# The divided input projection of a streaming encoder step: its two accumulators in PSUM tiles of their own

## Chip, cores and metric

One NeuronCore of one Trainium2 chip. The metric is the device time of one execution in microseconds (us).

## What is computed

One step of a one-layer encoder for 512 new frames of one stream (the prompt) and 32 frames of a running stream. All 544 frames go through the kernel together. The part that matters here is the input projection and the recurrence that it feeds:

```python
def token_mixer(x, s0, lat_past, kr_past, blk, lb, w_in, ...):
    proj = x @ w_in                                   # (544, 2048) @ (2048, 4928)
    hq, hf, hi, hg, cq, ckv, kr = jnp.split(proj, SPLITS, axis=-1)
    f = lb + (1.0 - lb) * jax.nn.sigmoid(hf.astype(jnp.float32))
    o_h, s_new = hgrn2_recurrence(heads(hq), heads(1.0 - f), heads(jnp.log(f)), heads(hi), s0, blk)
    o_h = rms_norm(o_h, ...) * jax.nn.silu(hg)
    ...                                               # MLA attention from cq, ckv, kr
    return jnp.concatenate([o_h, o_a], axis=-1) @ w_out, ...
```

Then follow layer norms and a ConvFFN with 5632 channels. There are eight heads of 128 columns in each of hq, hf, hi and hg. Everything is in fp32.

## The kernel before, in words

Every fp32 factor is split into a high part and a low part (`wh`, `wl` for weights; `aH`, `aL` or the pairs in `sums` for the activations), and a product is made of three matmuls: high by high, high by low, low by high. ACT makes the high part of a weight by a rounding copy, DVE the low part by a subtraction.

The projection of heads 0 and 1 is plain. Heads 2 to 7 use a divided form: a group `c` stands for 256 output columns (hq and hf of a head, or hi and hg of a head) and 544 frames. Columns, frames and the 2048 inner rows are each cut in two, and seven products of half size take the place of eight, in the order `ORDER = ("11", "s1", "s2", "s4", "s3", "12", "22")`. There are 12 groups and so 84 products. A product is 8 steps of k by 3 matmuls, each 128x128 weights by 272 columns (`NI`), all at line L773. Before some products DVE forms a difference of two raw weight blocks (`form`, L711); `begin` (L716, ACT) and `complete` (L721, DVE) make a product's high and low parts two products ahead.

The function `divided(c, a, b, after)` multiplies one group. It has two accumulators, x and y. Products 11, s2, s3 and 22 are added up in x, s1 and s4 in y, and 12 opens y afresh; the accumulator therefore alternates from product to product: x y x y x y x. After each product one 128x272 reading of its accumulator is needed (`take`): four of the seven are copies by ACT (L758), three are additions to what is there by DVE (L761), after which the forget gate or the output gate goes on (`after`, L789, L790, L798, L799). A `take` isn't issued at once. It is put in `later`, and `settle()` issues it in the middle of the next product, after its k = 3, just ahead of `complete`. After each half product the generator yields.

x and y are two slices of one tile of `main_tile()`: a tile of 128 x 1024 fp32 in the PSUM pool `psm`, which has two such tiles. Each group asks for a tile, so the groups take turns. The other PSUM of this stage is the pool `psg`: one tile `sw` of 1024 columns and two tiles `s1` of 512 columns, for the recurrence.

Between the half products ("slots") stand the steps of the recurrence, placed by `turns`: per head one generator `levels(h)` of nine steps and one `finish(h)` of eleven. `levels` begins with `Kp` and `Qp` on DVE (L815, L816), then the matmuls L821 (from `Kp`) and, level by level, L838 and L841 or L836 on PE, L842, L850 and L854 on DVE, L844 on POOL. `finish` has transposes and matmuls L870, L880, L892, L902, L904 on PE, L885, L887 and L894 on DVE, and at its end a chain: a square on ACT (L907), a sum and a scale on DVE (L911, L912), a power on POOL (L913), a multiplication on DVE (L916), five transposes on PE (L921), the result on DVE (L923, L925).

All this is inside `manual_schedule(engines=MANUAL)`: PE, DVE and ACT run their instructions in the order in which the code issues them. The framework puts in the semaphore waits. DMAs are issued on SP: four raw weight blocks of 512 KB for each group (L701). When the groups are over, `wo_tiles` takes two tiles of the same pool `psm` for the output projection (`out_first`, L118), whose instructions the framework places itself.

Of the kernel before, what the change touches and what calls it, by code (L numbers as in the profile page):

```python
# [42 lines left out]
NI = T // 2  # L43
# [16 lines left out]
def tile_encoder_step(ctx, tc, xp, xs, w_in, w_in4, w_kr, w_q_b, w_kv_b, w_out, w_up, w_gate, w_down, w_down2,  # L60
# [31 lines left out]
    def main_tile():  # L92
        return psm.tile([P, 1024], F32, name="main", tag="main")
# [54 lines left out]
    def pair_half(ps, j):  # L148
        n = H_[j].stop - H_[j].start
        return [ps[:, 512 * t:512 * t + n] for t in range(2)]  # L150
# [213 lines left out]
    with tc.tile_pool(name="mp", bufs=1) as mp, tc.tile_pool(name="psa", bufs=4, space=PSUM) as psa:  # L364
# [67 lines left out]
        c = {}  # L432
# [207 lines left out]
    with tc.tile_pool(name="gp", bufs=1) as gp, tc.tile_pool(name="psg", bufs=1, space=PSUM) as psg:  # L640
# [83 lines left out]
        def operand(name, k):  # L724
            if name in sums:
                return part(name, k, 0), part(name, k, 1)
            kg, j = {"11": (k, 0), "s3": (k, 1), "12": (HK + k, 0), "22": (HK + k, 1)}[name]
            return aH[kg][:, H_[j]], aL[kg][:, H_[j]]
# [4 lines left out]
        def begin(n):  # L733
            if n < len(products):
                ws_of[n] = products[n][0].high(products[n][1])

        def complete(n):

            if n < len(products):
                ws_of[n] = products[n][0].low(ws_of[n])  # L740
                if n + 1 < len(products):
                    products[n + 1][0].form(products[n + 1][1])

        def settle():
            now, later[:] = later[:], []
            for f in now:
                f()

        def divided(c, a, b, after):

            ps = main_tile()
            x, y = ps[:, :NI], ps[:, 512:512 + NI]
            t0, t1 = H_

            def take(name, out):
                kept = {"11": a[:, t0], "s1": b[:, t1], "s2": b[:, t0], "22": a[:, t1]}.get(name)
                if kept is not None:
                    A.activation(kept, out, AF.Copy)  # L758
                else:
                    z = {"s4": b[:, t0], "s3": b[:, t1], "12": a[:, t0]}[name]  # L760
                    V.tensor_tensor(out=z, in0=z, in1=out, op=ALU.add)  # L761
                    if name != "12":
                        after(z)

            for i, name in enumerate(ORDER):
                n = 7 * (c - N_PLAIN) + i
                begin(n + 2)
                wh, wl = ws_of.pop(n)
                out = x if name in ("11", "s2", "s3", "22") else y
                for k in range(HK):  # L770
                    oh, ol = operand(name, k)
                    for q, (ww, aa) in enumerate(((wh, oh), (wh, ol), (wl, oh))):
                        PE.matmul(out, ww[:, k * P:(k + 1) * P], aa, start=name in ("11", "s1", "12") and k == 0 and q == 0,  # L773
                                  stop=k == HK - 1 and q == 2, skip_group_check=True)
                    if k == 3:
                        settle()
                        complete(n + 2)
                        yield
                later.append(lambda name=name, out=out: take(name, out))
                yield  # L780
# [4 lines left out]
        def divided_qf(h):  # L785
            q, f = hq[h], hf[h] = proj_tile(), proj_tile()

            def forget(z):
                A.activation(z, z, AF.Sigmoid)  # L789
                A.activation(z, z, AF.Identity, bias=lb[:, h:h + 1], scale=oml[:, h:h + 1])  # L790
            yield from divided(2 * h, q, f, forget)

        def divided_ig(h):
            i, g = hi[h], hgate[h] = proj_tile(), proj_tile()

            def gate(z):
                e = gp.tile([P, 2, NI], F32, name="sg", tag="sg")[:, 0]
                A.activation(e, z, AF.Sigmoid)  # L798
                later.append(lambda: V.tensor_tensor(out=z, in0=z, in1=e, op=ALU.mult))  # L799
            yield from divided(2 * h + 1, i, g, gate)  # L800
# [143 lines left out]
        for n in range(2):  # L944
            begin(n)
            complete(n)
        last_finish = finish(HEADS - 1)
        with tc.manual_schedule(engines=MANUAL):

# [50 lines left out]
    def acc_tile():  # L1000
        seq[0] += 1
        if seq[0] % 2:
            return main_tile()
        return psA.tile([P, 1024], F32, name="acc", tag="acc")
# [349 lines left out]
    for g in (5, 6, 7):  # L1354
# [3 lines left out]
        if g < 7:  # L1358
            ps = pair_half(acc_tile(), 0)
# [218 lines left out]
    with tc.manual_schedule():  # L1578
# [26 lines left out]
        ps = pair_half(acc_tile(), 0)  # L1605
# [81 lines left out]
        for p in range(2, BP):  # L1687
            x = Pair(p)
# [553 lines left out]
```

## Time and profile before

| | |
|---|---|
| median of 3 runs | 2451.21 us (2450.78 to 2453.78) |
| the profiled execution | 2452.24 us, span 2450.5 us |
| PE busy | 2354.3 us (96% of the span) |
| DVE busy | 1812.1 us (74%) |
| ACT busy | 1045.2 us (43%) |
| POOL busy | 191.5 us (8%) |
| matmuls of L773 | 380.7 to 776.0 us |

How to read the rows: PE is TensorE's matmul, PEld its weight load, DVE is VectorE, ACT is ScalarE, POOL is GpSimd, SP issues the DMAs. A row of the timeline has the start in us, the length in us, engine, line, operation, what is written <- what is read, shapes and how many were merged; brackets hold the idle time of the engine ahead of it and what ended it. A row of waits reads "who <- for whom: total us, times, longest us". A row of the windows has, for a stretch of time, its length and then the busy time and number of instructions of PE, PEld, DVE, ACT and POOL, then the granted share of TensorE's clock, DMA's share and GB/s. Tile names are shown without numbers, so both tiles of `psm` are called `main`. Matmuls overlap: each row of L773 is some 0.29 us long, and the next begins some 0.13 us after it.

### The profile page before, as it was taken

To read this page: it belongs to the slowest core of one execution; us is meant where nothing else is said; L and a number is where in the kernel's file an instruction comes from. 1 tells how busy PE (TensorE), PEld (TensorE's weight loads), DVE (VectorE), ACT (ScalarE), POOL (GpSimd) and SP (SyncE) were. 2 spreads that over 40 slices of the span, in tenths; PEclk is the share of its full clock that TensorE was granted. 3 is DMA by queue.
4 is the path that set the end of the run, shared out by engine and by line. 5 is a ranking of instruction groups with operands and counts; after the bars stand their busy time and mean duration, and the time that the engine had idled before them with its cause. 6 is when DMAs were issued, how large, how long until landed. Compare 5 with 4: busy or idle time off the path is not lost.

```text
span 2450.5 us, 44455 instructions
## 1 busy us (share of the span) xinstructions
PE 2354.3 (96%) x18462; PEld 2317.5 (95%) x18462; DVE 1812.1 (74%) x2447; ACT 1045.2 (43%) x1615; POOL 191.5 (8%) x219
## 2 busy tenths in 40 slices
PE   6999999888899999989999999999999999999997
PEld 6999999888888999989999999999999999999996
DVE  7445577666667546799888888888777888888566
ACT  4244433333334224656555555555444433333234
POOL 4010020111111020000000000000000100000023
PEclk9999999999999999999999999999999999999998
DMA  7232163222224433644535253534333874633322
GB/s 231 91 97 65 62 200 95 70 77 69 73 76 145 170 101 124 204 135 161 174 119 184 102 191 112 177 127 164 117 117 118 313 300 170 224 133 94 115 70 74
DMA packets 131914, 333.21 MB, mean 136 GB/s; under 512 B 11904, under 2 KB 64896, under 8 KB 127104
## 3 DMA queue, kind: packets, MB, share of 16 engines
q1 hardware_dynamic: 122448, 286.91, 35.6%
q0 software_dynamic: 5040, 39.00, 4.0%
q10 hardware_dynamic: 4224, 4.46, 0.5%
q8 instruction: 145, 2.38, 0.4%
q14 instruction: 57, 0.47, 0.1%
HBM read 272.78 MB, written 56.15 MB: 134 GB/s over the span
## 4 chain that ended last, share of the span: by engine, by line
PE 75%; DVE 6%; ACT 2%; issue 2%; POOL 0%; DMA 0%; ACTq 0%; SPq 0%; DVEq 0%
PE main L1217 20%; PE acc L1217 16%; PE main L773 9%; PE main L1245 8%; PE main L118 7%; PE acc L1245 6%; PE acc L118 5%; PE s L838 1%; DVE wl L1169 1%; ACT hproj L758 1%; ACT wh L716 0%; DVE wl L721 0%; DVE hproj L761 0%; ACT zb L1337 0%; PE sw L902 0%
## 5 line engine op out<-in xcount | busy, mean ns | idle before, releaser
L1168 ACT ACTIVATE wh<-raw 128x1024 fp32r<-128x1024 f32 x340 | 359.9, 1059 | 415.0 <-DVE raw L1161 134.4
L1169 DVE TENSOR_TENSOR wl<-raw,wh 128x1024 fp32r<-128x1024 f32 x340 | 415.8, 1223 | 133.9 <-ACT wh L1168 133.0
L1217 PE MATMUL main<-op,wh 128*128 128x272 f32 x1408 | 265.7, 288 | 0.0
L1217 PE MATMUL acc<-ops,wh 128*128 128x272 f32 x1344 | 255.7, 289 | 4.3 <-DVE ops L1298 4.3
L1217 PE MATMUL main<-ops,wh 128*128 128x272 f32 x1344 | 254.2, 287 | 0.0
L1217 PEld LDWEIGHTS main<-op,wh 128*128 128x128 f32 x1408 | 221.0, 188 | 0.0
L1217 PEld LDWEIGHTS acc<-ops,wh 128*128 128x128 f32 x1344 | 212.1, 189 | 4.6 <-DVE ops L1298 4.6
L1217 PEld LDWEIGHTS main<-ops,wh 128*128 128x128 f32 x1344 | 211.0, 188 | 0.0
L1217 PE MATMUL main<-op,wl 128*128 128x272 f32 x704 | 203.1, 288 | 0.9 <-DVE wl L1169 0.9
L1217 PE MATMUL acc<-ops,wl 128*128 128x272 f32 x672 | 194.3, 289 | 0.0
L1217 PE MATMUL main<-ops,wl 128*128 128x272 f32 x672 | 193.8, 288 | 0.2 <-DVE wl L1169 0.2
L118 PE MATMUL main<-aL,wh 128*128 128x272 f32 (+2 forms) x768 | 180.1, 292 | 4.6 <-POOL aL L269 4.6
L118 PE MATMUL main<-aH,wh 128*128 128x272 f32 (+2 forms) x768 | 183.4, 296 | 1.1 <-ACT x L267 0.7
L118 PE MATMUL main<-aH,wl 128*128 128x272 f32 (+2 forms) x768 | 178.9, 291 | 0.0
L107 DVE TENSOR_TENSOR wl<-raw,wh 128x1024 fp32r<-128x1024 f32 (+2 forms) x80 | 89.9, 1127 | 102.9 <-ACT wh L106 97.9
L1217 PE MATMUL acc<-op,wh 128*128 128x272 f32 x832 | 159.8, 290 | 1.6 <-DVE eg L1441 1.6
L1168 ACT ACTIVATE wh<-rawl 128x1024 fp32r<-128x1024 f32 x93 | 98.5, 1060 | 105.8 <-DVE rawl L1161 42.1
L1161 DVE TENSOR_TENSOR raw<-raw,raw 128x1024 f32<-128x1024 f32 x114 | 139.2, 1221 | 1.8 <-DMA raw<-in_w_up 0.2
L773 PE MATMUL main<-aH,wh 128*128 128x272 f32 x384 | 118.2, 308 | 22.6 <-DVE hproj L761 22.6
L1169 DVE TENSOR_TENSOR wl<-rawl,wh 128x1024 fp32r<-128x1024 f32 x93 | 113.8, 1223 | 32.7 <-ACT wh L1168 32.4
L106 ACT ACTIVATE wh<-raw 128x1024 fp32r<-128x1024 f32 (+2 forms) x80 | 75.5, 949 | 140.2 <-PE acc L118 65.6
L118 PEld LDWEIGHTS main<-aL,wh 128*128 128x128 f32 x768 | 129.6, 191 | 5.8 <-POOL aL L269 5.7
(421 smaller groups left out, 6162.0 us busy)
## 6 DMA issues: line engine op xcount, KB each, us to landing
raw<-in_w_in SPq DMA_DIRECT2D x76, 512.0 KB, 3.6
raw<-in_w_up SPq DMA_DIRECT2D x72, 512.0 KB, 4.6
raw<-in_w_gate SPq DMA_DIRECT2D x72, 512.0 KB, 4.0
raw<-in_w_down SPq DMA_DIRECT2D x71, 512.0 KB, 4.1
raw<-in_w_out SPq DMA_DIRECT2D x40, 512.0 KB, 3.5
opd<-ohl SPq DMA_DIRECT2D x16, 1088.0 KB, 5.5
ops<-opd POOLq DMA_DIRECT2D x16, 1088.0 KB, 9.7
opd<-ohl SPq DMA_DIRECT2D x16, 816.0 KB, 6.4
```

The costliest lines, as they stand in the source:

```text
L106: A.activation(dst(hv), src(rv), AF.Copy)
L107: V.tensor_tensor(out=dst(lv), in0=src(rv), in1=dst(hv).bitcast(F32), op=ALU.subtract)
L118: PE.matmul(ps, ww[:, wcols[0]:wcols[1]], aa[:, hs[j]], start=first and i == 0, stop=last and i == 2, skip_group_check=True)
L758: A.activation(kept, out, AF.Copy)
L773: PE.matmul(out, ww[:, k * P:(k + 1) * P], aa, start=name in ("11", "s1", "12") and k == 0 and q == 0, stop=k == HK - 1 and q == 2, skip_g ...
L838: PE.matmul(ps[:, j * 64:(j + 1) * 64], Kp[:, a:b], Qv[:, j * bt:(j + 1) * bt, 1, :], start=True, stop=True)
L1161: V.tensor_tensor(out=out, in0=a, in1=b, op=ALU.subtract)
L1168: A.activation(wh, src, AF.Copy)
L1169: V.tensor_tensor(out=wl, in0=src, in1=wh.bitcast(F32), op=ALU.subtract)
L1217: PE.matmul(ps, ww[:, k * P:(k + 1) * P], aa, start=self.first and k == 0 and i == 0, stop=k == n - 1 and i == 2, skip_group_check=True)
L1245: PE.matmul(banks[:, 512 * u:512 * u + NI], ww[:, (u * n + k) * P:(u * n + k + 1) * P], aa, start=self.first and k == 0 and i == 0, stop=k ...
```

## The change

The two accumulators become the first 272 columns of two tiles. The tiles are asked for once, ahead of the first group, and kept for all of them. x of group c lies in tile c % 2 and y in the other one. As a group has seven products, the last of a group and the first of the next lie in different tiles.

```diff
@@ -748,8 +748,7 @@
 
         def divided(c, a, b, after):
 
-            ps = main_tile()
-            x, y = ps[:, :NI], ps[:, 512:512 + NI]
+            x, y = (banks[(c + i) % 2][:, :NI] for i in range(2))
             t0, t1 = H_
 
             def take(name, out):
@@ -944,6 +943,7 @@
         for n in range(2):
             begin(n)
             complete(n)
+        banks = [main_tile() for i in range(2)]
         last_finish = finish(HEADS - 1)
         with tc.manual_schedule(engines=MANUAL):
```

## The prediction

> **What bounds the kernel now.** I read the page first, then the stage in which the changed lines run, then its waits, then its timeline. The page:
>
> ```profile
> PE 2354.3 (96%) x18462; PEld 2317.5 (95%) x18462; DVE 1812.1 (74%) x2447; ACT 1045.2 (43%) x1615; POOL 191.5 (8%) x219
> ...
> PE main L1217 20%; PE acc L1217 16%; PE main L773 9%; PE main L1245 8%; PE main L118 7%; PE acc L1245 6%; PE acc L118 5%; PE s L838 1%; DVE wl L1169 1%; ACT hproj L758 1%; ACT wh L716 0%; DVE wl L721 0%; DVE hproj L761 0%; ACT zb L1337 0%; PE sw L902 0%
> ```
>
> PE is busy 96% of the span, so only its idle time or its work can be saved. The last of these lines is the chain of work that ended last: the multiplications of the divided projection (L773) hold 9% of it, and the two lines that empty their accumulators (L758 on ACT, L761 on DVE) stand in it too. An emptying line in this chain means that PE waited for it. The stage, from the view of busy time by windows, and then its waits (total, times, longest):
>
> ```profile
> core 0: us, PE busy (x) PEld busy (x) DVE busy (x) ACT busy (x) POOL busy (x), PEclk, DMA share, GB/s
> 380.70:776.00 395.30, 353.33 (x2749) 338.85 (x2748) 271.90 (x389) 143.44 (x214) 53.10 (x49) 0.99 0.27 83
> ```
>
> ```profile
> ACT hproj L758 <- PE main L773: 77.6, 26, 4.7
> DVE hproj L761 <- PE main L773: 25.1, 13, 4.3
> PE main L773 <- DVE hproj L761: 22.6, 23, 2.5
> PE main L773 <- ACT hproj L758: 17.9, 31, 1.0
> ```
>
> PE is idle for 395.30 - 353.33 = 42.0 us of the stage, and 22.6 + 17.9 = 40.5 us of that ends when L761 or L758 has read an accumulator: 54 stalls in 84 products. The other two rows show the reverse wait, of the reading engine for PE. One stall, in the timeline:
>
> ```profile
> 733.72 0.29 PE L773 MATMUL main<-aL,wh 128*128 128x272 f32 x1
> ...
> 733.84 0.29 PE L773 MATMUL main<-aH,wl 128*128 128x272 f32 x1
> 734.17 0.44 DVE L761 TENSOR_TENSOR hproj<-hproj,main 128x272 f32<-128x272 f32 x1 [4.23 <-PE main L773]
> 734.52 1.22 DVE L721 TENSOR_TENSOR wl<-raw,wh 128x1024 fp32r<-128x1024 f32 x1
> ...
> 734.66 0.39 PE L773 MATMUL main<-aH,wh 128*128 128x272 f32 x1 [0.53 <-DVE hproj L761]
> ```
>
> The row at 733.84 is the last matmul of a product's first half (k = 3). By the code the DVE row adds the accumulator of the product before, the other half of the same tile. It starts only when that first half ends, and PE's second half starts only when it is done. Neither touches the other's columns: x is in columns 0 to 271, y in 512 to 783. So the wait is one of the shared tile. The counterproof is the first product of a group, whose `settle` reads the old group's tile:
>
> ```profile
> 743.84 0.38 ACT L758 ACTIVATE hproj<-main 128x272 f32<-128x272 f32 x1
> 743.86 0.28 PE L773 MATMUL main<-aL,wh 128*128 128x272 f32 x1
> ```
>
> There ACT reads one `main` while PE writes another, and PE's row has no idle time ahead of it.
>
> **The change, part by part.** No instruction, DMA or wait on data is added or removed; the order on each engine's queue stays, since the stage is ordered by hand. Three things change.
>
> *1. The wait in the middle of a product goes.* The price of one: from 733.84 to 734.66 is 0.82 us where 0.13 is usual (733.72 to 733.84), so 0.69 is lost, 0.16 more than the 0.53 that counts as idle (a matmul's row is 0.29 long, but they start every 0.13). All 54 stalls: 40.5 + 54 x 0.16 = 49.1 us, the most that this can return.
>
> Not all of it returns, because PE then arrives early at other waits. The stage repeats with the heads, so I walk one head, from the matmuls L821 to the next head's L821:
>
> ```profile
> 683.63 0.60 PE L821 MATMUL sw<-hproj,Kp 128*128 128x128 f32 x4
> ...
> 749.39 1.20 PE L821 MATMUL sw<-hproj,Kp 128*128 128x128 f32 x10
> ```
>
> ```profile
> 683.60:749.40 65.80, 58.08 (x458) 55.66 (x457) 44.79 (x63) 22.39 (x33) 8.75 (x8) 1.00 0.22 67
> ```
>
> ```profile
> 740.44 0.40 PE L773 MATMUL main<-aH,wh 128*128 128x272 f32 x1 [2.51 <-DVE hproj L761]
> ...
> 747.78 0.52 PE L773 MATMUL main<-s,wh 128*128 128x272 f32 x2 [0.49 <-ACT hproj L758]
> ```
>
> Idle in this head: 65.80 - 58.08 = 7.72 us in ten stalls. The last three are those at 734.66, 740.44 and 747.78; the seven before them hold 7.72 - 0.53 - 2.51 - 0.49 = 4.19 idle, 4.19 + 7 x 0.16 = 5.3 lost. For these I find nothing that is late next. In the levels, where DVE has most to do, it waits for PE ahead of each level's product:
>
> ```profile
> 695.80 0.44 DVE L842 TENSOR_TENSOR Qp<-Qp,tot 128x272 f32<-128x272 f32 x1 [0.65 <-PE s L841]
> ...
> 700.77 0.44 DVE L842 TENSOR_TENSOR Qp<-Qp,tot 128x272 f32<-128x272 f32 x1 [1.74 <-PE s L841]
> ```
>
> Each of these waits shrinks by one stall (0.49 to 0.60 idle, 0.65 to 0.76 lost), and the smallest, 0.65, is just used up by it. If that cover were gone, a level would cost what DVE has too much. So 5.3 us return.
>
> The last three stalls, 3.53 idle and 4.0 lost, return only in part. Here DVE runs a chain of its own that ends in the next head's `Kp`, which L821 needs:
>
> ```profile
> 739.22 0.82 DVE L916 TENSOR_TENSOR sqg<-sw,r 128x640 f32<-128x640 f32 x1 [1.28 <-POOL r L913]
> ...
> 743.97 2.46 DVE L721 TENSOR_TENSOR wl<-raw,wh 128x1024 fp32r<-128x1024 f32 x2 [0.26 <-ACT wh L716]
> ...
> 747.48 0.44 DVE L815 TENSOR_SCALAR Kp<-hproj 128x544 f32<-128x544 f32 x1
> ```
>
> From the end of L916 (740.04) to the end of `Kp` (747.92) there are 7.88 us with one idle time, 0.26, in it; and L916 itself hangs on POOL and on a rounding (734.52) that follows the reading at 734.17 in the queue and so can start at most 0.35 earlier; I take 0.2. PE gets from L916's end to L821 in 749.39 - 740.04 = 9.35 us now, and after in no less than 7.88 + 0.05. So this end of the head returns 0.2 + 1.4 = 1.6 of 4.0 us. Late next are the transposes L921 (for L916, by about 1.2 us) and L821 (for `Kp`, by about as much).
>
> One head returns 5.3 + 1.6 = 6.9 us; the five alike (50 of the 54 stalls) 34.5. The other four stalls have 40.5 - 5 x 7.72 = 1.9 idle, 2.5 lost; of these 2.0 return. **Sum of part 1: 36.5 us.**
>
> *2. The same two accumulators serve every group.* A product's first matmul now waits for the reading of two products before, also across a group's end, where a fresh tile was taken. That reading is issued half a product earlier, 12 x 0.126 = 1.5 us ahead of the need, and no longer waits for PE. Where L921 stands at the group's end, ACT's reading (743.84 to 744.22) ends 4.2 us behind L916's end, held up in ACT's queue by a rounding that waits for DVE. PE would want that accumulator at 3.6 (L921, then 24 matmuls): 0.6 us of wait, but L821 has to wait for `Kp` anyway, so it costs nothing there. At the other group ends I count none. Bounds: nothing below, since a wait gains nothing; above, this line's one sequencer wait, for each of 84 products, 4.3 us:
>
> ```profile
> L773 PEldq EVENT_SEMAPHORE  x1: 51/51/51, 398.5 to 398.5; - x1
> ```
>
> I take 0, since the line's 54 waits of now made only this one such row.
>
> *3. The tiles after the stage.* The output projection's first tile was free early, and four of its matmuls filled PE before the stage had ended:
>
> ```profile
> L118 PE MATMUL main<-aH,wh x2: 290/340/390, 767.8 to 772.1; 128*128 128x272 f32 x2
> L118 PE MATMUL main<-aL,wh x2: 287/287/287, 772.2 to 772.3; 128*128 128x272 f32 x2
> ```
>
> Now the tile is held until the last group is read, and they follow. Cost at most 4 x 0.13 = 0.5 us, which I take. Weight loads follow the buffers' release, which comes earlier with the reading engines; DMA at a share of 0.27 covers them.
>
> **The clock.** Twice in the stage the granted clock halves after one of the 2.5 us stalls:
>
> ```profile
> 538.16:541.57 3.41, 1.58 (x12) 1.58 (x13) 2.77 (x4) 0.00 (x0) 0.57 (x1) 1.00 0.00 0
> 541.57:544.99 3.42, 3.42 (x18) 3.42 (x17) 2.83 (x5) 2.29 (x3) 0.00 (x0) 0.50 0.09 33
> 674.69:678.11 3.42, 3.42 (x18) 3.42 (x17) 2.81 (x5) 2.29 (x3) 0.00 (x0) 0.50 0.08 29
> ```
>
> PE was busy 1.58 of the 3.41 us before. Each half clock costs 3.42 / 2 = 1.7 us. With the long stall down to about 1.2 us no window of that length is half empty, so I take both as gone: 3.4 us. The Trainium skill, "TensorE: Matmul & The Clock Gate", section on the HAM clock gate, has the clock fall after an idle window of about 3.4 us; here it fell after a window with 1.58 us of work. By the page's rule these dips would not come from the stalls and would stay, the sum would be 36.0 and the time 2415; I go by the rows.
>
> **Sum.** 36.5 - 0.5 + 3.4 = 39.4 us. The profiled execution took 2452.24 us (span 2450.5), which gives 2412.8; the median of the runs shown, 2451.21, is 1.0 below it, so **2412 us** as the median.
>
> **Rivals.**
>
> *All of it returns* (49.1 + 3.4): about 2399. For it: L916 and `Kp` could come earlier if the readings ahead of them in DVE's queue shift more than I saw. Against it: the 7.88 us chain has 0.26 us of slack.
>
> *DVE is the bound wherever it ended a stall.* Then only ACT's stalls return, 17.9 + 31 x 0.16 = 22.9: 2428. For it: DVE is busy 271.9 of what would be about 356 us. Against it: the 1.74 us waits above, and 25.1 us in which DVE itself waits for the first halves.
>
> *The change doesn't do what it says*: the mid-product wait has another cause than the tile, and stays: 2451. Against it: the rows at 743.84.
>
> *Slower, by too few banks.* The stage falls from four halves of 512 columns in turn to two. If the readings come later than a product's start, every product waits. To lose, PE must wait more than 49.1 / 84 = 0.58 us on each of 84 products, that is, each reading must end over 1.5 + 0.58 us after the `settle` that issues it. A reading takes 0.38 to 0.44; only the one behind L916 came 2.5 late, in five of 84. At 1 us each, 84 - 49 = 35 us slower: 2486. The Trainium skill speaks for this one: "Perfetto Trace Analysis", section Matmul Optimizations, wants all eight PSUM banks in use. No row here shows a product that waited for want of a bank.
>
> **How the numbers follow.** My forecast 0.76 (0.2 of it with the clock's dips left), all returns 0.06, DVE the bound 0.12, no effect 0.03, slower 0.03. The likeliest case alone runs from 2403 (the end of the head returns half of what I withheld, 5 us, and some more comes from the tail) to 2424 (no clock dip goes, 4.3 us of sequencer waits, a few us in the later stages, whose clock dips shift). The range takes in most of the DVE case: 2402 to 2428. Less than 0.2%, 4.9 us, can't be told from no change here. Faster 0.94, the same 0.03, slower 0.03.
>
> **What would show it.** Right: between the two halves of a product PE no longer waits for L758 or L761, and their idle total falls from 40.5 to below 5 us; L758's 77.6 us of waiting for L773 shrinks; PE waits instead for L916 at L921 and for L815 at L821, about 2.4 us a head; a head is 59 us long instead of 65.8; no half clock between the stage's ends. Wrong: the stalls move to the first matmul of a product, or the levels' matmuls (L838) begin to wait for `Qp` or `Kp`, or the later stages take back what this one gives.

## The result, and the profile after

The changed kernel takes 2407.98 us (median, 2407.74 to 2409.69), beside 2450.99 us of the kernel before on the same chip: a ratio of 0.9826, with an interval of 0.9809 to 0.9843. It is 43.0 us faster; forecast were 39.2 (2451.21 to 2412). The profiled execution took 2409.69 us, with a span of 2407.9. From the second statement of `divided` on, the line numbers are one lower: L773 is now L772, L758 and L761 are L757 and L760, L815 is L814, L821 is L820, L916 is L915, L921 is L920.

The page of the changed kernel, busy time and chain:

```profile
PE 2341.2 (97%) x18462; PEld 2314.0 (96%) x18462; DVE 1809.7 (75%) x2447; ACT 1044.0 (43%) x1615; POOL 192.3 (8%) x219
...
PE main L1217 20%; PE acc L1217 16%; PE main L772 8%; PE main L1245 8%; PE main L118 7%; PE acc L1245 6%; PE acc L118 5%; PE s L837 1%; DVE wl L721 1%; DVE raw L711 1%; DVE wl L1169 1%; ACT wh L716 0%; ACT zb L1337 0%; PE sw L820 0%; PE sw L901 0%
```

The two reading lines are no longer named in the chain; in their place stand the lines that form and split the weights on DVE (L711, L721). The stage and one head of it (from L820 to the next head's L820), by windows with the columns of before; first the stage of the kernel before. Its last matmul of L773 ends at 775.2 us, not at the 776.0 of the table and of the prediction's window, so it is shown to that end:

```profile
380.80:775.20 394.40, 352.80 (x2746) 338.44 (x2744) 271.10 (x387) 142.64 (x212) 53.00 (x49) 0.99 0.27 84
```

```profile
380.40:729.50 349.10, 337.13 (x2739) 332.28 (x2738) 267.31 (x385) 139.62 (x210) 52.26 (x49) 1.00 0.30 94
647.20:705.50 58.30, 56.10 (x455) 55.27 (x456) 44.40 (x64) 22.20 (x34) 8.83 (x8) 1.00 0.27 84
```

The stage is 45 us shorter, PE's idle time in it has gone from 394.40 - 352.80 = 41.6 to 349.10 - 337.13 = 12.0 us, and no half clock is left in it. The head has 2.2 us of idle time where it had 7.7. Who waits for whom in the stage:

```profile
ACT hproj L757 <- PE main L772: 28.0, 13, 4.8
...
PE sw L920 <- DVE sqg L915: 7.5, 6, 1.3
...
PE sw L820 <- DVE Kp L814: 2.5, 5, 0.5
...
PE main L772 <- ACT hproj L757: 2.0, 5, 0.4
```

The 54 waits of PE for a reading in the middle of a product, 40.5 us, are gone; five others have come, 2.0 us, which lie at the start of a product. No wait for L760 remains. The new waits are the two that the prediction named, for L915 and for L814. In the timeline of one head's end (PE, then DVE):

```profile
637.73 0.29 PE L772 MATMUL main<-aH,wl 128*128 128x272 f32 x1
639.29 0.76 PE L920 MATMUL sw<-ident,sqg 128*128 128x128 f32 x5 [1.27 <-DVE sqg L915]
...
643.46 0.52 PE L772 MATMUL main<-s,wh 128*128 128x272 f32 x2 [0.39 <-ACT hproj L757]
...
647.25 1.27 PE L820 MATMUL sw<-hproj,Kp 128*128 128x128 f32 x10 [0.50 <-DVE Kp L814]
```

```profile
638.40 0.82 DVE L915 TENSOR_TENSOR sqg<-sw,r 128x640 f32<-128x640 f32 x1 [1.28 <-POOL r L912]
...
646.67 0.43 DVE L814 TENSOR_SCALAR Kp<-hproj 128x544 f32<-128x544 f32 x1
```

From L915's end (639.22) to L820 (647.25) there are 8.03 us; the prediction set "no less than 7.88 + 0.05". The waits add up to 1.27 + 0.39 + 0.50 = 2.2 us a head, where about 2.4 was forecast.

### The profile page after: what moved, and what is told of

The parts are those of the page before. It is cut to its first block, busy times and chain, and to the rows that moved or that the text cites. A ratio compares the mean times of both kernels' runs of the same rounds, so it can differ in the third digit from the quotient of the medians.

```text
span 2407.9 us, 44481 instructions
## 1 busy us (share of the span) xinstructions
PE 2341.2 (97%) x18462; PEld 2314.0 (96%) x18462; DVE 1809.7 (75%) x2447; ACT 1044.0 (43%) x1615; POOL 192.3 (8%) x219
## 4 chain that ended last, share of the span: by engine, by line
PE 74%; DVE 7%; ACT 2%; issue 1%; POOL 0%; DMA 0%; ACTq 0%; DVEq 0%
PE main L1217 20%; PE acc L1217 16%; PE main L772 8%; PE main L1245 8%; PE main L118 7%; PE acc L1245 6%; PE acc L118 5%; PE s L837 1%; DVE wl L721 1%; DVE raw L711 1%; DVE wl L1169 1%; ACT wh L716 0%; ACT zb L1337 0%; PE sw L820 0%; PE sw L901 0%
## 5 line engine op out<-in xcount | busy, mean ns | idle before, releaser
L1168 ACT ACTIVATE wh<-raw 128x1024 fp32r<-128x1024 f32 x340 | 359.9, 1059 | 415.5 <-DVE raw L1161 133.9
L1169 DVE TENSOR_TENSOR wl<-raw,wh 128x1024 fp32r<-128x1024 f32 x340 | 415.7, 1223 | 134.7 <-ACT wh L1168 133.8
L1217 PE MATMUL main<-op,wh 128*128 128x272 f32 x1408 | 265.7, 288 | 0.0
L1217 PE MATMUL acc<-ops,wh 128*128 128x272 f32 x1344 | 256.8, 289 | 4.7 <-DVE ops L1298 4.7
L1217 PE MATMUL main<-ops,wh 128*128 128x272 f32 x1344 | 254.2, 287 | 0.0
L1217 PEld LDWEIGHTS main<-op,wh 128*128 128x128 f32 x1408 | 221.0, 188 | 0.0
L1217 PEld LDWEIGHTS acc<-ops,wh 128*128 128x128 f32 x1344 | 213.1, 190 | 5.0 <-DVE ops L1298 5.0
L1217 PEld LDWEIGHTS main<-ops,wh 128*128 128x128 f32 x1344 | 211.0, 188 | 0.0
L1217 PE MATMUL main<-op,wl 128*128 128x272 f32 x704 | 203.1, 288 | 0.9 <-DVE wl L1169 0.9
L1217 PE MATMUL acc<-ops,wl 128*128 128x272 f32 x672 | 194.8, 290 | 0.0
L1217 PE MATMUL main<-ops,wl 128*128 128x272 f32 x672 | 193.8, 288 | 0.2 <-DVE wl L1169 0.2
L1217 PE MATMUL acc<-op,wh 128*128 128x272 f32 x832 | 159.7, 290 | 1.4 <-DVE eg L1441 1.4
L721 DVE TENSOR_TENSOR wl<-raw,wh 128x1024 fp32r<-128x1024 f32 x84 | 102.9, 1224 | 50.9 <-ACT wh L716 50.8
L716 ACT ACTIVATE wh<-raw 128x1024 fp32r<-128x1024 f32 x84 | 88.6, 1055 | 117.9 <-DVE raw L711 111.9
```

The lines of the kernel that those rows point to most:

```text
L716: A.activation(wh, self.src, AF.Copy)
L721: V.tensor_tensor(out=wl, in0=self.src, in1=wh.bitcast(F32), op=ALU.subtract)
L1168: A.activation(wh, src, AF.Copy)
L1169: V.tensor_tensor(out=wl, in0=src, in1=wh.bitcast(F32), op=ALU.subtract)
L1217: PE.matmul(ps, ww[:, k * P:(k + 1) * P], aa, start=self.first and k == 0 and i == 0, stop=k == n - 1 and i == 2, skip_group_check=True)
```

## The experiments

Each is the changed kernel with the edit shown, unless it says otherwise. "A head" is the time from the first matmul from `Kp` (L820) to the same of the next head; it is 58.27 us in the changed kernel (588.98 to 647.25), 65.76 before without a clock dip (a stretch of half granted clock) and 67.34 with one. The kernels ran on three chips, on which the kernel before took 2450.8 to 2452.1 us.

**The tiles apart from the order.** In two kernels every reading is issued at the start of the next product, not in its middle: once with the shared tile of before, once with the tiles of their own. On each engine these two have the same order; only the tiles differ.

```diff
                 n = 7 * (c - N_PLAIN) + i
+                settle()
                 begin(n + 2)
...
                     if k == 3:
-                        settle()
                         complete(n + 2)
```

The shared tile (from the kernel before):

> The kernel before, x and y in one tile, with settle moved from the middle of a product to its start. Theory (PE waits because the reading and the product share a tile, wherever the reading stands): the waits move to the first matmul of each product and stay 0.5 us or more each, 30 to 72 of them; 2440 to 2470 us. Rival (the wait belongs to the place in the middle, to what else is issued there): it goes away with the place, about 2410 us.

It took 2526.17 us, ratio 1.0302 [1.0287, 1.0318]. The waits went where they were expected, to a product's first matmul, but their size was far off:

```profile
PE main L774 <- DVE hproj L761: 72.1, 31, 5.7
PE main L774 <- ACT hproj L758: 19.7, 25, 1.4
```

56 waits, 91.8 us. The longest, in DVE's row and PE's:

```profile
569.13 0.82 DVE L916 TENSOR_TENSOR sqg<-sw,r 128x640 f32<-128x640 f32 x1 [1.28 <-POOL r L913]
569.87 0.43 DVE L761 TENSOR_TENSOR hproj<-hproj,main 128x272 f32<-128x272 f32 x1
```

```profile
570.45 0.57 PE L774 MATMUL main<-aH,wh 128*128 128x272 f32 x1 [5.68 <-DVE hproj L761]
```

In the shared tile PE may begin a product only when the reading of the product before has run, and that stands behind whatever its engine's queue holds: here L916, which waits for POOL. The half product that PE had in hand in the kernel before, while the reading waited its turn, is gone. The expectation counted the reading's own length and not its queue. It also left out the clock, which is lower here. The stage by windows, with the shared tile and then, from the kernel that follows, with tiles of their own:

```profile
380.40:851.80 471.40, 375.33 (x2749) 361.59 (x2747) 275.04 (x388) 140.67 (x213) 48.58 (x49) 0.93 0.22 70
```

```profile
382.30:752.30 370.00, 340.67 (x2739) 335.19 (x2738) 266.66 (x384) 140.09 (x210) 50.74 (x49) 0.99 0.28 89
```

Tiles of their own, same order:

> The changed kernel with settle at the start of each product instead of the middle. Theory (with tiles of their own no reading holds PE, and the wait of 0.40 us at the first matmul of s1 between heads is covered by the wait for Kp behind it): the 0.40 us waits go, L820 waits longer for Kp by as much, the time is that of the changed kernel, 2408 +- 3 us. Rival (the reuse of an accumulator across a group's end costs what its wait shows): 5 x 0.40 = 2 us less, 2406; rival (a reading ahead of the product makes DVE and ACT wait at the head of their queues for PE): 5 us slower or more, 2413.

It took 2429.28 us, ratio 0.9907 [0.9891, 0.9924]. With an equal order on the engines, the tiles are worth 97 us here. By the two rows of windows the stage is 101 us shorter: PE has 67 us less of idle time (29.3 beside 96.1) and is busy 35 us less, at a mean granted clock of 0.99 beside 0.93. But the forecast was 2408, and it missed by 21; of its rivals, the one that expected 5 us or more of loss came nearest. But for one wait of 0.8 us, PE does not wait for the readings; it waits more for what DVE makes:

```profile
PE sw L920 <- DVE sqg L915: 14.4, 7, 2.6
PE sw L820 <- DVE Kp L814: 7.6, 6, 1.3
PE s L837 <- DVE totk L849: 5.6, 5, 1.1
```

Three more kernels look for the cause. In the first, only ACT's four copies are issued early; in the second, only DVE's three additions, with the sigmoids on ACT that follow two of them; the third is the changed kernel again, on the chip of these two.

```diff
-                later.append(lambda name=name, out=out: take(name, out))
+                (ahead_of if name in ('11', 's1', 's2', '22') else later).append(...)   # early copies
+                (ahead_of if name in ('s4', 's3', '12') else later).append(...)         # early additions
```

(`ahead_of` is a second list, issued at a product's start.)

> The changed kernel, but the four products that ACT copies out of PSUM (11, s1, s2 and 22) are read at the start of the next product; the three that DVE adds (s4, s3, 12) stay in its middle. The version that reads all seven early took 2429 us, 21 more than the changed kernel. Theory: that loss comes from the additions on DVE, because the sigmoids that stand behind them on ACT are pulled ahead of ACT's rounding of the next pieces. By it this one gives 2407 us (2404 to 2410), with the 0.40 us wait at product s1 of each group gone. Rival: any early reading holds up the queue that it stands in, the copies too; by it 2415 us or more, and waits of PE for the rounded pieces or for the subtraction that gives Kp grow.

> The changed kernel, but the three products that DVE adds (s4, s3 and 12) are read at the start of the next product; the four that ACT copies stay in its middle. Theory (the sigmoids behind the additions, pulled ahead of ACT's rounding, make the 21 us): as with all seven read early, 2428 us (2424 to 2433), a head near 61 us, PE waiting over 2 us a head for the rounded square. Rival (the copies are what hold the queue up): 2408 us (2405 to 2412). If both kinds share it: between the two, 2413 to 2423.

> The changed kernel again, unchanged, on the chip of the two others, so that they can be compared within a few us: 2408 us (2406 to 2411) by every theory.

Measured: early copies 2409.49 us, ratio 0.9831 [0.9817, 0.9846]; early additions 2422.68, 0.988 [0.9863, 0.9896], just below the span that was expected of them and inside the one given for both kinds sharing the loss; the changed kernel 2407.88, 0.9821 [0.9806, 0.9835]. So 14.8 of the 21 us come with the additions and 1.6, no more than the executions differ by, with the copies; the rest, some 5 us, shows only where both are early, and that is a comparison across chips. The last of this series keeps the additions early and puts the sigmoids back into the product's middle:

```diff
                     if name != "12":
-                        after(z)
+                        later.append(lambda: after(z))
```

> The changed kernel with DVE's three additions (s4, s3, 12) read at the start of the next product, as in the version that took 2422.7 us, but the sigmoids and scales on ACT that follow two of them stay in the middle of that product. Theory: the 15 us of that version come from the sigmoids, which stand ahead of ACT's rounding of the next pieces; without that 2408 us (2405 to 2411), a head 58.3 us, ACT's wait at the sigmoid for the addition (48 us in the stage) back at about 18. Rival: the additions themselves, ahead of other work in DVE's queue, cost it: 2420 us or more. Between 2412 and 2419 both have a part.

It took 2407.73 us, ratio 0.9822 [0.9808, 0.9836], with heads of 58.29 us. So the additions cost nothing where they stand, and the 15 us come with the sigmoids. The multiplication on DVE that follows the sigmoid of the output gate (L804, which waits 5.3 us in all for it in the kernel with early sigmoids) is issued later together with it; no run takes the two apart. The waits of ACT and DVE for one another, first with the additions and sigmoids early, then with the sigmoids back in the middle (there L803 is the sigmoid of the output gate, L794 that of the forget gate, L765 the addition, L804 the multiplication):

```profile
ACT sg L803 <- DVE hproj L765: 48.2, 11, 6.6
...
ACT hproj L794 <- DVE hproj L765: 24.9, 7, 4.2
...
DVE wl L721 <- ACT wh L716: 64.9, 45, 3.1
```

```profile
ACT sg L803 <- DVE hproj L804: 15.1, 5, 3.0
...
ACT hproj L794 <- DVE hproj L765: 5.5, 7, 0.8
ACT sg L803 <- DVE hproj L765: 2.9, 5, 0.6
...
DVE wl L721 <- ACT wh L716: 50.8, 28, 3.2
```

ACT's waits at the output gate's sigmoid fall from 48.2 to 15.1 + 2.9 = 18.0 us, as expected (about 18). DVE's waits at L721 fall by 14 us, from 64.9 to 50.8.

And the same place of a head in both: ACT and then DVE with early sigmoids, and last ACT with the sigmoids back in the middle:

```profile
612.28 0.43 ACT L803 ACTIVATE sg<-hproj 128x272 f32<-128x272 f32 x1 [6.59 <-DVE hproj L765]
612.62 1.04 ACT L716 ACTIVATE wh<-raw 128x1024 fp32r<-128x1024 f32 x1
```

```profile
611.83 0.42 DVE L765 TENSOR_TENSOR hproj<-hproj,main 128x272 f32<-128x272 f32 x1
...
613.69 1.23 DVE L721 TENSOR_TENSOR wl<-raw,wh 128x1024 fp32r<-128x1024 f32 x1 [0.51 <-ACT wh L716]
```

```profile
600.54 1.06 ACT L716 ACTIVATE wh<-raw 128x1024 fp32r<-128x1024 f32 x1 [4.96 <-DVE raw L711]
602.19 0.43 ACT L803 ACTIVATE sg<-hproj 128x272 f32<-128x272 f32 x1 [0.58 <-DVE hproj L765]
```

The sigmoid waits in ACT's queue for DVE's addition, and the rounding (L716) stands behind it. With the sigmoid first, the rounding begins 12.8 us into the head (612.62 less 599.83); with the rounding first, 10.9 us (600.54 less 589.66). DVE then waits for it at L721, and is late for all that follows. DVE's queue had waited for ACT and ACT's for DVE, with PE at the end of both.

**The roles.** In one kernel each group begins with `settle()`, with the roles in turn as in the change; in the other this is so too, but x is always the one tile and y the other.

```diff
                 n = 7 * (c - N_PLAIN) + i
+                if i == 0:
+                    settle()
                 begin(n + 2)
...
-            x, y = (banks[(c + i) % 2][:, :NI] for i in range(2))
+            x, y = (banks[i][:, :NI] for i in range(2))          # only with fixed roles
```

> The changed kernel with a settle at the start of each group only, so that ACT reads the last product of a group ahead of the rounding that waits for DVE. Theory: PE's 0.40 us wait at the first matmul of s1 between heads goes, L820 waits as much longer for Kp, a head stays 58.3 us long, 2408 +- 1.5 us. Rival (the reuse of an accumulator across a group's end costs what it shows): a head of 57.9, 2 us less, 2406.

> The changed kernel with x always in the first tile and y always in the second, and a settle at the start of each group, since the last product of a group and the first of the next then share a tile. Theory (the shared tile made the mid-product waits; the change of roles only spares a wait at the 11 group ends): the 54 mid-product waits stay away; at the 6 group ends inside a head PE waits once for ACT's reading, about 0.75 us each, 4.5 us; at the 5 between heads PE waits for L915 anyway. 2408 + 4.5 = 2412 us. Rival (the change of roles is what brings the gain): most of the 43 us is lost, 2430 us or more.

Roles in turn: 2407.59 us, ratio 0.9821 [0.9807, 0.9834], heads of 58.13 us. Fixed roles: 2411.94, 0.984 [0.9826, 0.9855], heads of 58.86. Both times are what the theories gave (2408 and 2412). The first removes the 0.39 us wait at product s1, and nearly all of it comes back at `Kp`, so that a head gains 0.14 us:

```profile
PE sw L922 <- DVE sqg L917: 7.4, 6, 1.3
PE sw L822 <- DVE Kp L816: 5.0, 5, 1.0
```

With fixed roles the last product of a group and the first of the next share a tile, and this wait is added to the same two:

```profile
PE main L774 <- ACT hproj L757: 2.9, 6, 0.5
```

So the turn of the roles is worth 0.7 us a head; the tiles of their own bring nearly all the gain.

**What is late next.** Three kernels go for the waits that remain. In the first, the transposes L920 are issued one slot later, so that a finish has twelve steps; in the second, the sum, scale and power (L910 to L912) are issued in the slot of the square, one earlier; both for heads 1 to 6. In the third, `Kp` is made on ACT. A fourth has the second edit (the run e4 of its expectation) and the third together.

```diff
             A.activation(sq, o3, AF.Square)
-            yield
+            inner = 0 < h < HEADS - 1
+            if not inner:
+                yield                                            # sum, scale and power one slot earlier
...
             G.tensor_tensor(out=r1, in0=r0, in1=nhalf, op=ALU.pow)
+            if inner:
+                yield
             yield
...
+            if 0 < h < HEADS - 1:
+                yield                                            # only in the first: transposes one slot later
             tp = sw_tile()
...
-            V.tensor_scalar(out=Kp, in0=f, scalar1=-1.0, scalar2=1.0, op0=ALU.mult, op1=ALU.add)
+            A.activation(Kp, f, AF.Identity, bias=ones[:, 0:1], scale=-1.0)   # Kp on ACT
```

> The changed kernel with the five transposes L920 and what follows them in a finish one slot later, for heads 1 to 6. Theory (DVE's chain to the next Kp sets the pace between heads, not PE's wait in front of L920): the 1.27 us of waiting at L920 go, but L922 and L924 now stand behind the wait of L721 for ACT's rounding, the chain to Kp grows by about 1.0 us a head, and L820 waits longer: 2408 + 5 = 2413 us (2409 to 2416). Rival (the wait in front of L920 is worth what it shows): 5 x 1.27 = 6.4 us less, 2402.

It took 2410.39 us, ratio 0.9835 [0.9821, 0.985]; a head is 59.0 us, 0.7 longer. The wait at the transposes leaves the heads, and two others take its place, of which only the one for `Kp` was expected:

```profile
PE main L772 <- DVE hproj L760: 8.5, 5, 1.7
PE sw L820 <- DVE Kp L814: 6.3, 6, 1.2
```

PE now runs ahead into a product whose accumulator has not been read, since the reading (L760) stands behind L915 in DVE's queue.

> The changed kernel with the sum, scale and power of a finish (L910, L911, L912) issued right behind the square, one slot earlier, for heads 1 to 6; the multiplication L915 and all later steps keep their slots. Theory (what the change still withholds hangs on DVE's chain from the square to the next Kp): L915 ends some 2.1 us earlier after the square, PE's waits at L920 (1.27), at the first matmul of s1 (0.40) and at L820 (0.50) nearly go, 2.1 us for each of 5 heads, 10.5 us: 2397 us. Rival (the chain is as long because DVE is full there): L915 moves, but Kp doesn't, 0 to 3 us: 2405 to 2408.

> The changed kernel with Kp = 1 - f made by ACT (0.6 us, in a hole of ACT's queue some 2 us ahead) instead of DVE. Theory (L820 waits for Kp at the end of DVE's chain): the 0.50 us wait at L820 goes, a head of 57.8 instead of 58.3, 2.5 us less, 2405.5. Rival (the next wait, for Qp at L837, takes its place): a head of 58.2, 2408.

> The early sum of the run e4 and Kp on ACT together. Theory (they shorten one chain at two places and PE has nothing left to wait for between heads): a head of 56.45 - 0.5 = 55.95 us, and against the run e4 2.5 us less, about 2397. Rival (PE then waits for Qp at L837 or for weights): as e4, 2399.6.

The early sum took 2399.62 us, ratio 0.9788 [0.9773, 0.9802], with heads of 56.4 us, 1.8 less; 2.1 less was forecast, since PE's wait for `Kp`, 0.50 us a head, was to go and stayed. `Kp` on ACT took 2400.53, 0.9796 [0.9783, 0.981]: more than forecast, since a head fell by 0.73 us (to 57.54) where the wait had counted as 0.50 of idle time, and the first two heads shrank as well. Both together took 2392.99 us, ratio 0.9763 [0.9748, 0.9778], the fastest of all: 15 us below the changed kernel and 4 below the forecast. One head of it by windows:

```profile
634.50:690.20 55.70, 55.65 (x458) 55.21 (x457) 44.01 (x63) 22.92 (x34) 8.79 (x8) 1.00 0.26 84
```

PE's idle time is 0.05 us of 55.70. A head is 10.06 us shorter than before the change, so the early arrivals that DVE had withheld were to be had.

## Why the prediction was right, and where its sizes were off

The measured numbers are those of the two profiled executions, from the rows of L821 and L820 and the stage's last matmul.

- *The wait of the shared tile in the middle of a product.* Right: all 54 waits are gone, and the pair with equal order shows that it is the tile and not the order.
- *The price of a stall, 0.69 us.* Too small by 0.10. The prediction added 0.16 for the overlap that is lost, but not that the first matmul behind a stall is itself longer: 0.39 us in the quoted row of 734.66 where its neighbours have 0.29. In the kernel with `Kp` on ACT, a stall with 0.50 of idle time was worth 0.73 to a head, and 0.50 + 0.16 + 0.10 = 0.76. The most that the change could return was then 40.5 + 54 x 0.26 = 54.5 us, not 49.1.
- *A head returns 6.9 us.* It returned 65.76 - 58.27 = 7.5. Seven stalls gave 4.19 + 7 x 0.26 = 6.0, not 5.3: the matmul that began 733.84 - 683.63 = 50.21 us into its head begins 691.46 - 647.25 = 44.21 us into it in the changed kernel. The end of the head gave 7.5 - 6.0 = 1.5, with 1.6 forecast. The five heads gave 40.6 us, 3.2 of it clock, so 37.4 rather than 34.5. (The row at 734.52, which the prediction calls a rounding, is the subtraction of L721.)
- *What is late next.* Right in place and size, 2.2 us of waits a head. The early sum, which only changes the order on DVE, returned 1.8 us of a head. With `Kp` on ACT as well no wait is left, but that edit also takes an instruction of 0.43 us a head off DVE. So most of the bound was the order in which DVE did its work.
- *Other stalls, 2.0 us.* The first two heads are 2.2 us shorter and the end of the stage 1.8, but some 1.0 of the latter is work that has only moved: four matmuls of the output projection and four of five transposes (L870) that began ahead of the last half product now follow it. That leaves 3.0.
- *Bank reuse, 0.* Right: a wait of 0.39 came, and its removal returned 0.14 a head. With transposes that do not hold PE up it becomes 1.7 us, so the cover is thin.
- *The fillers, -0.5, and the later stages, 0.* From the stage's end to the span's end the execution before took 1675.3 us and the one after 1678.4, which gives 3.1 us back. 1.0 of it is the moved work, where 0.5 was forecast, since the transposes were left out. Another 1.4 come at one place, where the half clock lasts 3.41 us in the execution before and 6.83 in the one after: a matmul of L1217 ahead of it starts at 1069.15 us before and at 1025.02 after, 44.13 us earlier, and one behind it at 1092.74 and 1050.01, only 42.73 earlier. The windows of this place, before and after:

```profile
1080.88:1087.71 6.83, 6.43 (x40) 6.43 (x41) 4.71 (x5) 2.59 (x5) 0.00 (x0) 0.75 0.73 273
```

```profile
1036.48:1043.31 6.83, 5.75 (x25) 5.75 (x26) 4.50 (x4) 2.51 (x6) 0.00 (x0) 0.50 0.66 250
```

  Of the twelve profiled executions with two tiles, seven have 6.83 us there and five 3.41, so the two tiles do not decide it. The remaining 0.7 is not traced. The changed kernel run again took 1674.9 us for the same stretch, and 2.5 of the 3.4 us between these two executions come at another such window, at half clock in the first and at full clock in the second:

```profile
951.14:957.97 6.83, 6.83 (x32) 6.83 (x33) 4.12 (x7) 2.50 (x3) 1.78 (x1) 0.50 0.64 230
```

```profile
950.78:957.61 6.83, 5.92 (x49) 5.63 (x48) 4.88 (x8) 2.95 (x4) 1.78 (x1) 1.00 0.74 264
```

- *The clock, 3.4.* Right: the two heads with a dip were 1.6 us longer each, and no half clock is left in the stage. The rule of the Trainium skill, "TensorE: Matmul & The Clock Gate", section on the HAM clock gate, by which, as the prediction applies it, these dips would have stayed, does not agree with that.

The sum: heads 37.4, the other stalls 3.0, the clock 3.2, the tail without the moved work -2.1, and 1.1 by which the execution after was ahead before the first head's L820 (310.05 beside 311.11), where nothing was changed: 42.6 us, as are the spans (2450.5 to 2407.9). So the forecast of 39.2 was low by the restarts (2.9 in the heads, 1.0 elsewhere). That the later tail and the earlier start, which nothing here ties to the change, partly cancel is chance.

Of the rivals, too few banks is refuted as a mechanism of this kernel: PE waits 2.0 us in all for an accumulator. The rule of the Trainium skill, "Perfetto Trace Analysis", section Matmul Optimizations, to use all eight banks, has at most these 2.0 us to win here in this stage. DVE as the bound wherever it ended a stall is refuted: its 22.6 us of stalls in L773 are gone, and PE's new waits for DVE, at L920 and L820, are 7.5 + 2.5 = 10.0 us. That all returns came true only with the two further edits.

## What to carry to other kernels

Two halves of one PSUM tile were one thing to the waits that the framework set here, so an accumulator that is read while its neighbour is written belongs in a tile of its own; the sign of it is a matmul in the middle of an accumulation that waits for the reading of another. When such a wait is taken away, follow the next late result to its engine's queue and move that one instruction ahead, and look at what stands behind a new early one: a sigmoid that waits for DVE ahead of a rounding that DVE needs, with the multiplication behind it, cost 15 us. Price a stall of PE by idle time, lost overlap and the slower first matmul: here 0.26 us on top of the idle time.

## What was unexpected of the hardware

- The first matmul after a stall took 0.39 us instead of 0.29, and the next began 0.23 us after it instead of 0.13 (734.66 and 734.89 in the kernel before).
- The clock. Past the first 30 us of the fourteen profiled executions, every window of 3.41 us at full clock (laid end to end from each change of the clock) with 1.61 us of PE work or less was followed by half clock; of those with 1.65 to 2.62 us some were and some were not; none with more was. The windows ahead of the two rows at 951 us, in the changed kernel and in the same again, show how little decides:

```profile
947.73:951.14 3.41, 1.77 (x15) 1.55 (x14) 3.30 (x7) 1.20 (x3) 0.00 (x0) 1.00 1.02 393
```

```profile
947.37:950.78 3.41, 1.78 (x15) 1.55 (x14) 3.30 (x7) 1.15 (x3) 0.00 (x0) 1.00 1.01 387
```

  The same work, at the same place: after the first the clock halved for 6.83 us, after the second it did not. So 2.5 us of a comparison of two single executions of this kernel can be chance at this place alone. The section of the Trainium skill named above has the clock fall after an idle window; here one that was over half busy could do.
